# The two output products by Strassen's method, and all 22 contraction tiles of the FFNs' second products

## The chip, the cores and the metric

The kernel runs on one core of a Trainium2 chip. TensorE (PE) multiplies; VectorE (DVE), ScalarE (ACT) and GpSimd (POOL) work elementwise; SyncE (SP) and POOL issue DMAs. The metric is device time of one execution in microseconds (us), lower is better.

## The reference

One decoder layer on 512 tokens of width 1024, in fp32, batch 1: four sublayers, each followed by a normalisation of a scaled residual.

```python
def _swiglu(h, w_in, w_out):                   # w_in 1024 x 5632, w_out 2816 x 1024
    gate, up = jnp.split(h @ w_in, 2, axis=-1)
    return (jax.nn.silu(gate) * up) @ w_out

def _parallel_mixer(...):
    ...                                        # o: 4 HGRN2 heads of 128, p: 4 pooling groups of 128
    merged = jnp.concatenate([o, p], axis=-1)
    return merged @ w_out                      # 1024 x 1024

def _memory_attention(h, mem, wq, wk, wv, wo):
    q = (h @ wq)...; k = (mem @ wk)...; v = (mem @ wv)...
    p = jax.nn.softmax(s * XA_HEAD_DIM ** -0.5, axis=-1)
    o = jnp.einsum('bhsm,bmhd->bshd', p, v).reshape(b_, s_, D_MODEL)
    return o @ wo                              # 1024 x 1024

h = LN(ALPHA * h + 0.5 * _swiglu(h, ...))      # FFN1
h = LN(ALPHA * h + _parallel_mixer(h, ...))    # mixing
h = LN(ALPHA * h + _memory_attention(h, ...))  # attention into 256 memory tokens
h = LN(ALPHA * h + 0.5 * _swiglu(h, ...))      # FFN2
```

## The kernel before

**Precision.** Every fp32 operand is split in two parts: `split` (L66) lets ACT cast it to `hi` and DVE make `lo` as the difference; `mm3` and its kin then take three matmuls, hi x hi, hi x lo, lo x hi. So every tile that is to be multiplied costs one ACT and one DVE instruction of its size. `wblock` (L74) does this for a block of weights: SP loads 128 x 1024 values into a `raw` buffer (7 of them), and the two parts go to `q` buffers (7 of them, so three and a half blocks) or, with `stay`, to a large buffer (names `whi_`, `wlo_`, `ws_`).

**Order.** The program is written in one order; the framework that builds it places the instructions of each engine, follows the buffers' and data's dependencies and sets the semaphores. Each engine then works through its own list in that order. The lists are fixed before the run.

**Stages.** FFN1 (names `f1`), mixing, its output product (`mo`) with the memory keys around it (`pk`, `wk` blocks), values and queries of the attention, attention, its output product (`xo`), FFN2 (`f2`). The 512 tokens are four tiles of 128 (`h0` to `h3`), the residual is kept there, and after an output product each tile is normalised (`ln_tile`: statistics and the two linear steps on DVE, `rstd` on POOL) and transposed on PE (`trh`, L195) for the next stage.

**Output products before.** `out_gemm` (L209) takes 8 contraction tiles in 4 blocks for each half of the 1024 columns; its left side comes split already (`mg0` to `mg3`, `oT0` to `oT3`), because the steps that make it split it: the pooling groups (`pool_out`), the merge of the heads (`og`, `ot`), the attention's values (`values`). Each product is 192 matmuls of 128x512. The second half is done tile by tile, so that a tile's addition, normalisation and transposes run beside the next tile's matmuls.

**Second products of the FFNs before.** `strassen_gemm` (L317) takes Strassen's (Winograd's) form over tokens (two halves) x columns (two halves) x contraction. Seven products, in the order b11, t1, t2, b21, b22, t3, t4: the left sides are quarters `a11`, `a12`, `a21`, `a22` of the activation or sums of them made by `combine` on DVE, each split by `left` when its turn comes; the right sides are blocks of the weights (b11, b21, b22) or sums (t1 to t4) read back from DRAM. Results gather in six PSUM tiles (`u`, `v`, `w`, two each), and `add` puts them into `h`. 20 of the 22 contraction tiles go this way, in 5 blocks a product (`KB1`, `KB2`); the last two are multiplied directly by `rest` (blocks `ws`, left side `gs`), 48 matmuls between the products' ends and the additions.

**Sums.** `Sums` (L268) makes t1 to t4 in DRAM by DMAs of POOL's queue: a copy, then an accumulating DMA. Where they are issued is set by a small POOL instruction on a weight block's `hi` (`seen`): in FFN1 `step` issues four to six every other group of the first product; for FFN2 `spread` spreads its 40 over the 50 weight blocks of mixing and attention. All are issued before the second product begins.

## Time and profile before

| | |
|---|---|
| median of 3 runs | 1042.48 us (1042.39 to 1042.53) |
| the profiled execution | 1043.13 us |
| its span | 1041.4 us, 1.73 us lie around it |
| granted TensorE clock | 0.997 |
| output product of mixing, first transpose of the merge to last key | 493.3 to 557.5 us |
| attention's last value product to the first FFN2 products' end | 650.9 to 722.1 us |
| second product of FFN2 | 925.5 to 1031.0 us |

A row of the stretches gives: from and to, length, then busy us (instructions) of PE, weight loads (PEld), DVE, ACT, POOL, then the granted clock, the share of the DMA engines and GB/s. A row of waits gives: engine, what was to be written and the line, from whom it came, us in total, times, the longest. A row of the timeline gives: start, us, engine, line, operation, out<-in, shape, and in square brackets the idle time before it with its releaser. The rows of the chain give start, us, engine, what.

```profile
q1 hardware_dynamic: 38592, 128.25, 36.9%
q0 software_dynamic: 4480, 41.95, 15.9%
f2t<-in_w2out POOLq DMA_DIRECT2D x30, 512.0 KB, 6.6
```

These are the DMA queues (packets, MB, share of 16 engines' span): SP's loads above, the sums of POOL's queue below; an action of the sums for FFN2 takes 6.6 us from issue to landing.

### The profile page before, as it was taken

How to read it: one execution, taken by the hardware profiler on the slowest of the kernel's cores; microseconds unless marked ns; L12 is line 12 of the kernel's file. 1: busy time of each engine (PE TensorE's matmuls, PEld its weight loads, DVE VectorE, ACT ScalarE, POOL GpSimd, SP SyncE). 2: the span in 40 equal slices, each digit the busy share in tenths (PEclk: the TensorE clock that was granted, in tenths of full speed). 3: DMA queues.
4: the chain of work that ended last, by engine and by line, in shares of the span. 5: the costliest groups of instructions: out<-in, count | busy, mean ns of one | idle time of the engine just before them, and what ended most of it. 6: DMA issues, size and time to landing. Idle time of an engine off the chain costs nothing. (4 is left out here: it accounts for less than half of the span.)

```text
span 1041.4 us, 17704 instructions
## 1 busy us (share of the span) xinstructions
PE 1025.7 (98%) x6910; PEld 929.4 (89%) x6910; DVE 825.4 (79%) x1334; ACT 504.3 (48%) x857; POOL 95.0 (9%) x167
## 2 busy tenths in 40 slices
PE   9999999999999999999999999999999999999996
PEld 7999999998887888879888988889999999988884
DVE  6999888789898545786786356589988888889795
ACT  5656555566554331334324345226555555566530
POOL 0112211200000111102303110010000000000000
PEclk9999999999999999999999999999999999999998
DMA  9377786585665446553929871403233332436751
GB/s 364 143 236 230 222 254 212 148 247 158 216 192 182 142 155 169 148 168 82 292 72 314 273 162 41 141 22 107 97 101 122 103 101 65 139 102 202 235 189 41
DMA packets 43300, 171.59 MB, mean 165 GB/s; under 512 B 6096, under 2 KB 7376, under 8 KB 40016
## 3 DMA queue, kind: packets, MB, share of 16 engines
q1 hardware_dynamic: 38592, 128.25, 36.9%
q0 software_dynamic: 4480, 41.95, 15.9%
q8 instruction: 54, 0.88, 0.3%
q10 hardware_dynamic: 144, 0.26, 0.1%
q14 instruction: 30, 0.25, 0.1%
HBM read 168.34 MB, written 44.04 MB: 204 GB/s over the span
## 5 line engine op out<-in xcount | busy, mean ns | idle before, releaser
L177 POOL TENSOR_TENSOR rstd<-ve,mhalf 128x1 f32<-128x1 f32 x16 | 14.8, 922 | 536.1 <-DVE ve L175 536.1
L538 PE MATMUL f1u<-xt,qf1s 128*128 128x256 f32 x480 | 60.7, 283 | 0.0
L538 PE MATMUL f2u<-xt,qf2s 128*128 128x256 f32 x480 | 60.7, 283 | 0.0
L538 PEld LDWEIGHTS f1u<-xt,qf1s 128*128 128x128 f32 x480 | 59.0, 192 | 0.0
L538 PEld LDWEIGHTS f2u<-xt,qf2s 128*128 128x128 f32 x480 | 59.0, 192 | 0.0
L68 DVE TENSOR_TENSOR wlo_wv<-raw_wv,whi_wv 128x1024 fp32r<-128x1024 f32 x12 | 14.7, 1224 | 23.8 <-PE pq L57 8.5
L538 PE MATMUL f1u<-xT,qf1a 128*128 128x256 f32 x240 | 32.1, 283 | 0.0
L538 PE MATMUL f2w<-xoT,qf2a 128*128 128x256 f32 x240 | 32.1, 283 | 0.0
L538 PE MATMUL f2u<-xoT,qf2a 128*128 128x256 f32 x240 | 32.1, 283 | 0.0
L538 PE MATMUL f1w<-xT,qf1a 128*128 128x256 f32 x240 | 32.1, 283 | 0.0
L538 PE MATMUL f1v<-xt,qf1s 128*128 128x256 f32 x240 | 30.7, 283 | 0.0
L538 PE MATMUL f1u<-xt,qf1a 128*128 128x256 f32 x240 | 30.6, 283 | 0.0
L538 PE MATMUL f1v<-xT,qf1s 128*128 128x256 f32 x240 | 30.4, 283 | 0.0
L538 PE MATMUL f2v<-xt,qf2s 128*128 128x256 f32 x240 | 30.4, 283 | 0.0
L538 PE MATMUL f2v<-xoT,qf2s 128*128 128x256 f32 x240 | 30.4, 283 | 0.0
L538 PE MATMUL f2u<-xt,qf2a 128*128 128x256 f32 x240 | 30.4, 283 | 0.0
L538 PEld LDWEIGHTS f1w<-xT,qf1a 128*128 128x128 f32 x240 | 30.3, 192 | 0.1
L538 PEld LDWEIGHTS f1u<-xT,qf1a 128*128 128x128 f32 x240 | 30.2, 192 | 0.0
L538 PEld LDWEIGHTS f2w<-xoT,qf2a 128*128 128x128 f32 x240 | 30.2, 192 | 0.0
L538 PEld LDWEIGHTS f2u<-xoT,qf2a 128*128 128x128 f32 x240 | 30.2, 192 | 0.0
L538 PEld LDWEIGHTS f1v<-xt,qf1s 128*128 128x128 f32 x240 | 29.6, 192 | 0.1
L538 PEld LDWEIGHTS f1u<-xt,qf1a 128*128 128x128 f32 x240 | 29.6, 192 | 0.0
(458 smaller groups left out, 3220.3 us busy)
## 6 DMA issues: line engine op xcount, KB each, us to landing
f1t<-in_w1out POOLq DMA_DIRECT2D x30, 512.0 KB, 8.2
f2t<-in_w2out POOLq DMA_DIRECT2D x30, 512.0 KB, 6.6
raw_f1t<-f1t SPq DMA_DIRECT2D x20, 512.0 KB, 4.1
raw_f2t<-f2t SPq DMA_DIRECT2D x20, 512.0 KB, 3.9
raw_f2g<-in_w2in SPq DMA_DIRECT2D x17, 512.0 KB, 3.7
raw_f2u<-in_w2in SPq DMA_DIRECT2D x17, 512.0 KB, 3.7
raw_f1u<-in_w1in SPq DMA_DIRECT2D x15, 512.0 KB, 7.2
raw_f1b<-in_w1out SPq DMA_DIRECT2D x15, 512.0 KB, 4.8
```

What stands on the lines that cost most here:

```text
L68: nc.vector.tensor_tensor(out=lo, in0=src, in1=hi.bitcast(F32), op=ALU.subtract)
L177: nc.gpsimd.tensor_tensor(out=rstd, in0=ve, in1=mhalf[:, 0:1], op=ALU.pow)
L538: nc.tensor.matmul(o, q[:, w, wsl], x[k][r], start=opens and k == 0 and n == 0, stop=ends and k == 3 and n == 2, skip_group_check=True)
```

## The change

`out_gemm` goes. `strassen_gemm` now takes its left side as a list of `groups` and its blocks from the sums' own lists `kb1`, `kb2`, and makes all three kinds of product: `mo` and `xo` (8 contraction tiles, 2 blocks a product) and the FFNs' second ones, there with all 22 tiles: 6 blocks a product, the last one half a block (`(10, 0)` and `(10, 1)`, 512 wide). `rest`, `ws` and `gs` go. An output product now has 168 matmuls of 128x512 where it had 192; an FFN's second product has 462 for 468. The left sides stay unsplit where they are made (`mgp` from the pooling, `mgh` from the merge, `oT0`, `oT1` copied by ACT from PSUM) and are split, and combined, inside.

```diff
-    mg = {q: b8([P, 2, 2, S], F32R, f"mg{q}") for q in (2, 3)}
+    mg = [None, b8([P, 4, S], F32, "mgp")]
...
-        ov = og.rearrange("p (a b n) -> p a b n", a=2, b=2)
-        for q in range(2):
-            split(ov[:, q], mg[q][:, :, 0, cs], mg[q][:, :, 1, cs])
-
-    X2 = out_gemm(a["wmixo"], KT, mslot, ALPHA, a["ln2_g"], a["ln2_b"], LN_EPS, "mo", order=[2, 3, 0, 1])
+    X2 = strassen_gemm([(mg[1], mg[0])], sums_mo, ALPHA, a["ln2_g"], a["ln2_b"], LN_EPS, "mo")
...
-            split(po, oT[:, j, 0, :], oT[:, j, 1, :])
+            nc.scalar.copy(out=OT[hd // 2][:, 2 * (hd % 2) + j, :], in_=po)
...
-    X3 = out_gemm(a["wo"], KT, lambda k: (OT[k // 2][:, k % 2, 0, :], OT[k // 2][:, k % 2, 1, :]),
-                  ALPHA, a["ln3_g"], a["ln3_b"], LN_EPS, "xo", ys=ys,
+    X3 = strassen_gemm([OT], sums_xo, ALPHA, a["ln3_g"], a["ln3_b"], LN_EPS, "xo", ys=ys,
...
+    FFN_BLOCKS = [0, 1, 4, 5, 8, (10, 0)], [2, 3, 6, 7, 9, (10, 1)]
```

The end of `strassen_gemm`: the direct blocks stood inside `rest`, between the Strassen products and the additions.

```diff
-        def rest(t, hf, ps, opens, scale):
-
-            block(t % 2, 0, ws[hf], gs[t // 2], ps, opens, True)
-            add(t, hf, ps, scale)
+        def stats_of(t, hf):
             nc.vector.bn_stats(stats[t][:, hf, :], h[t][:, hf * 512:hf * 512 + 512])
...
         for t in range(2):
             add(2 + t, 1, u[t], False, ALU.subtract)
-            rest(2 + t, 1, mm_ps(f"{name}x{t}"), True, False)
+            stats_of(2 + t, 1)
         for t in range(2):
             for i, x in enumerate(T4):
-                block(t, i, x, L, u[t], False, False)
-            rest(2 + t, 0, u[t], False, True)
+                block(t, i, x, L, u[t], False, i == nb - 1)
+            add(2 + t, 0, u[t], True)
+            stats_of(2 + t, 0)
             done(2 + t)
```

The sums: `mo` and `xo` need 16 DMAs each, an FFN 48 (where 40 were). Their order is now t1, t3, t2 of all blocks, then t4 of all. `step` in FFN1 no longer makes t4; what is left of a product's sums is put on a list at its start and issued one behind each weight block (`one_behind` in `wblock`), t4's beside the second product itself. The list for mixing and attention holds `mo`'s sums first, then `xo`'s and FFN2's in turn.

```diff
-        for f in behind:
-            f(hi)
+        one_behind(hi)
...
+    def one_behind(hi):
+        if todo_behind:
+            seen = st.tile([P, 1], F32, tag="seen", name="seen")
+            todo_behind.pop(0)(nc.gpsimd.tensor_tensor(out=seen, in0=hi[:, 0:1].bitcast(F32), in1=mhalf[:, 0:1],
+                                                       op=ALU.mult).ins)
...
+    todo_behind += sums_mo.actions()
+    todo_behind += [x for two in zip(sums_xo.actions(), sums2.actions()) for x in two]
+    todo_behind += sums2.actions()[len(sums_xo.actions()):]
```

The order on the engines changes at two places above all. The first is the start of mixing's output product on DVE. Before, behind the key splits, stood the merge, its splits and the rest of the weight blocks, and then one addition and one statistic for each tile (`wlo_mo1_3` is the last block of the second half):

```order
L887 SCALAR_TENSOR_TENSOR og_5332<-ot_5327,gn_3873,GS_4506 128x512 [waits PE_49]
L68 TENSOR_TENSOR ws_mo1_0_5486<-raw_mo1_0_5484,ws_mo1_0_5486 128x1024 [waits DMAHW5_49]
L68 TENSOR_TENSOR mg0_5147<-og_5332,mg0_5147 128x2x128 [waits Activation_49]
L68 TENSOR_TENSOR mg1_5148<-og_5332,mg1_5148 128x2x128 [waits Activation_49]
L68 TENSOR_TENSOR wlo_mo0_3_5422<-raw_mo0_3_5419,whi_mo0_3_5421 128x1024 [waits DMAHW1_49,PE_49]
L68 TENSOR_TENSOR ws_mo1_1_5495<-raw_mo1_1_5493,ws_mo1_1_5495 128x1024 [waits DMAHW6_49]
L68 TENSOR_TENSOR ws_mo1_2_5503<-raw_mo1_2_5501,ws_mo1_2_5503 128x1024 [waits DMAHW7_49]
L68 TENSOR_TENSOR wlo_mo1_3_5509<-raw_mo1_3_5506,whi_mo1_3_5508 128x1024 [waits DMAHW0_49,PE_49,Activation_49]
L243 SCALAR_TENSOR_TENSOR h0_266<-h0_266,mops00_5351 128x512 [waits PE_49]
L246 BN_STATS stats0_5338<-h0_266 128x6 [waits DVE_49]
```

Now the left sides, combinations and additions of each product stand between the weight blocks (`moa11` and `mos1` are left sides, L292 is `combine`, `mou` the PSUM tiles of product b11):

```order
L68 TENSOR_TENSOR moa110_5415<-mgp_4350,moa110_5415 128x4x256 [waits Activation_49]
L837 SCALAR_TENSOR_TENSOR mgh_5234<-ot_5399,gn_3953,GS_4592 128x4x128 [waits PE_49]
L292 TENSOR_TENSOR mos1_5418<-mgp_4350,mgh_5234 128x1024 [waits DVE_49]
L292 TENSOR_TENSOR mgp_4350<-mgp_4350 128x4x256 [waits DVE_49]
L68 TENSOR_TENSOR mos10_5464<-mos1_5418,mos10_5464 128x4x256 [waits Activation_49]
L323 SCALAR_TENSOR_TENSOR h0_266<-h0_266,mou0_5409 128x512 [waits PE_49]
L323 SCALAR_TENSOR_TENSOR h1_267<-h1_267,mou1_5410 128x512 [waits PE_49]
L68 TENSOR_TENSOR wlo_mot10_5472<-raw_mot10_5469,whi_mot10_5471 128x1024 [waits DMAHW0_49,Activation_49]
L68 TENSOR_TENSOR wlo_mot11_5494<-raw_mot11_5491,whi_mot11_5493 128x1024 [waits DMAHW1_49,Activation_49]
```

The first block of t1 moved behind five instructions of left sides and two additions; PE takes its `lo` in the third matmul of t1. The second place is the end of t3 in the same product. On DVE the addition that frees `mou0` stands behind both normalisations and t4's blocks:

```order
L180 SCALAR_TENSOR_TENSOR h1_267<-h1_267,rstd_5687,B_5659 128x512 [waits DVE_49,Pool_49]
L180 SCALAR_TENSOR_TENSOR h1_267<-h1_267,rstd_5687,B_5659 128x512 [waits DVE_49]
L68 TENSOR_TENSOR ws_mot40_5741<-raw_mot40_5739,ws_mot40_5741 128x1024 [waits DMAHW4_49]
L68 TENSOR_TENSOR wlo_mot41_5751<-raw_mot41_5748,whi_mot41_5750 128x1024 [waits DMAHW5_49,Activation_49]
L68 TENSOR_TENSOR moT0_5757<-trh00_5761,moT0_5757 128x2x128 [waits Activation_49]
L326 TENSOR_TENSOR h2_268<-h2_268,mou0_5409 128x512
```

and on PE, from the same point, the first matmul of t4 into `mou0` waits for DVE, between the transposes of tiles 0 and 1:

```order
L192 MATMUL trh00_5761<-ident_262,h0_266 128x128 [waits DVE_49,PE_49]
L192 MATMUL trh00_5761<-ident_262,h0_266 128x128 x3
L192 MATMUL trh01_5770<-ident_262,h0_266 128x128 [waits DVE_49,PE_49]
L192 MATMUL trh01_5770<-ident_262,h0_266 128x128 x3
L56 MATMUL pk_5894<-mT0_5091,whi_wk3_5887 128x256 [waits Activation_49]
L57 MATMUL pk_5894<-mT0_5091,whi_wk3_5887 128x256
L312 MATMUL mou0_5409<-ws_mot40_5741,moa220_5736 128x512 [waits DVE_49]
L192 MATMUL trh10_5779<-ident_262,h1_267 128x128 [waits DVE_49,PE_49]
```

Nothing like this wait stood in the plain product, whose PSUM tiles `mops` each took one tile's matmuls and were then read. The end of `xo` reads alike, with tile 1's transposes ahead of t4.

More of the change, by code (lines that the diff above doesn't have):

```diff
@@ L293, in add @@
                     nc.gpsimd.dma_start(self.T[p, b], x, accum_op=ALU.add, max_dma_last_dim=8192)
-        def spread(self, hi, over, count=[0]):
-            total = 8 * NB
-            n0, n1 = (total * (count[0] + i) // over for i in range(2))
-            count[0] += 1
-            for n in range(n0, min(n1, total)):
-                seen = st.tile([P, 1], F32, tag="seen", name="seen")
-                ins = nc.gpsimd.tensor_tensor(out=seen, in0=hi[:, 0:1].bitcast(F32), in1=mhalf[:, 0:1], op=ALU.mult).ins
-                if self.copies and (n % 2 == 0 or n < 4):
-                    self.copy(ins, engine=nc.gpsimd)
-                else:
-                    self.add(ins)
@@ L308, in step, with actions @@
-        def step(self, q, n):
+        def actions(self):
+            c, a, seq = len(self.copies), len(self.adds), []
+            while a:
+                if c and a - c < 4:
+                    seq.append(self.copy)
+                    c -= 1
+                else:
+                    seq.append(self.add)
+                    a -= 1
+            return seq
+        def step(self, q):
             seen = st.tile([P, 1], F32, tag="seen", name="seen")
             ins = nc.gpsimd.tensor_tensor(out=seen, in0=q[:, 0, 0:1].bitcast(F32), in1=mhalf[:, 0:1], op=ALU.mult).ins
-            for _ in range(3 if n in (2, 4) else 2):
-                self.add(ins)
-            for _ in range(3 if n < 4 else 2):
-                self.copy(ins, engine=nc.gpsimd)
@@ L851, in layer_kernel @@
         states.append(Sn)
-    for q in range(2):
-        mg[q] = b8([P, 2, 2, S], F32R, f"mg{q}")
+    mg[0] = b8([P, 4, S], F32, "mgh")
     os_ = []
```

193 lines of the change are left out of this document (73 added, 120 removed).

## The prediction

> **What bounds the kernel now.** Four views were read: first the shares of busy time on the page, then TensorE's waits over the whole span, then the chain that ended last, and last the table of stretches around the two output products (mixing and attention).
>
> ```profile
> PE 1025.7 (98%) x6910; PEld 929.4 (89%) x6910; DVE 825.4 (79%) x1334; ACT 504.3 (48%) x857; POOL 95.0 (9%) x167
> ```
>
> ```profile
> PE idle L106 <- DVE mhalf L160: 1.1, 1, 1.1
> PE trh L195 <- issue: 0.9, 1, 0.9
> PE f2u L356 <- DVE f2a L68: 0.7, 1, 0.7
> PE f1u L356 <- DVE f1a L68: 0.7, 1, 0.7
> PE first L56 <- ACT qx L67: 0.7, 1, 0.7
> PE trh L195 <- DVE h L183: 0.7, 1, 0.7
> PE po L56 <- ACT PT L67: 0.2, 1, 0.2
> ```
>
> ```profile
> 938.53 13.60 PE f2v L356 x60
> ...
> 1014.69 16.33 PE f2u L356 x72
> 1031.03 0.02 issue
> 1031.05 0.70 DVE h L367
> ```
>
> TensorE (PE) is busy for 1025.7 of 1041.4 us and waits for data 5.0 us in all; the rest of the gap is the 10.4 us tail after its last matmul (1031.0 to the end). So a matmul taken away is worth its own time, but only as long as no other engine becomes late in that stage. A 128x512 matmul goes every 13.60 / 60 = 0.2267 us.
>
> The stretches, PE first, then weight loads, DVE, ACT, POOL, granted clock, DMA share and GB/s: the mixing output product with what remains of the memory keys (first row), and the attention output product up to the first gate and value products of FFN2 (second row).
>
> ```profile
> 493.30:557.50 64.20, 64.17 (x362) 54.99 (x361) 50.96 (x88) 22.56 (x42) 17.36 (x27) 1.00 0.62 191
> 650.90:722.10 71.20, 70.50 (x416) 61.60 (x415) 54.39 (x84) 25.81 (x39) 3.96 (x4) 1.00 0.29 97
> 938.00:952.00 14.00, 14.00 (x64) 11.58 (x63) 14.00 (x16) 9.49 (x10) 0.00 (x0) 1.00 0.64 189
> ```
>
> Both stages are PE's, but DVE already has 51.0 of 64.2 us and 54.4 of 71.2 us. The third row, a Strassen product of FFN2, shows DVE busy all the time beside PE: there one product has 60 matmuls (13.6 us) to hide its splits and combinations behind.
>
> **The change part by part.** The sum is made against the profiled execution, 1043.13 us (span 1041.4 and 1.73 around it), which lies 0.65 above the median of the runs.
>
> PE: 60 matmuls of 128x512 go: 24 in each output product (192 to 168), 6 in each FFN (468 to 462). 60 x 0.2267 = 13.6 us. If nothing else became late, the result would be 1029.5.
>
> DVE's prices are starts of one instruction to the next, back to back (us from the start of the span, then us).
>
> ```profile
> 922.79 1.22 DVE L68 TENSOR_TENSOR wlo_f2b<-raw_f2b,whi_f2b 128x1024 fp32r<-128x1024 f32 x1
> 923.92 0.42 DVE L525 TENSOR_TENSOR f2g<-f2sg,f2u 128x256 f32<-128x256 f32 x1
> 924.25 2.36 DVE L68 TENSOR_TENSOR f2a<-f2g,f2a 128x1024 fp32r<-128x1024 f32 x2
> 926.52 1.22 DVE L339 TENSOR_TENSOR f2s<-f2g,f2g 128x1024 f32<-128x1024 f32 x1
> 938.20 1.28 DVE L367 SCALAR_TENSOR_TENSOR h<-h,f2u 128x512 f32<-128x512 f32 x2
> 939.39 1.22 DVE L68 TENSOR_TENSOR wlo_f2t<-raw_f2t,whi_f2t 128x1024 fp32r<-128x1024 f32 x1
> ```
>
> 1024 elements cost 923.92 - 922.79 = 1.13 to 1.14 us, 512 elements (939.39 - 938.20) / 2 = 0.60, 256 elements 0.33. A Strassen product of the output stages has two weight blocks (2.28), one left side (1.14), often a combination (1.14) and two additions out of PSUM (1.2): 5 to 7 us of DVE beside 24 matmuls, 5.44 us of PE. The plain product had 8 weight blocks and 8 additions.
>
> Mixing's output product adds 6 weight blocks (6.84), 7 left sides (7.98), 4 combinations (4.56) and 6 additions (3.6), and drops 8 splits of 256 elements (2.64): +20.3 us, 51.0 to 71.3. PE would need 64.2 - 5.4 = 58.8. DVE becomes the longer one there. The sum alone bounds the stage from below at about 71.3 less the 2 to 3 us of DVE work that can be done before it starts: +4.7 us against 64.2.
>
> What comes late is read from the order, walked by these prices from 493.3 (t = 0), with a transpose of a tile's half at 0.5 us as an estimate from its 128-wide matmuls. The start is where DVE is free of the merge's inputs in the trace:
>
> ```profile
> 491.50 0.69 DVE L874 TENSOR_TENSOR o<-o,rs 128x512 f32<-128x512 f32 x1 [1.12 <-POOL rs L873]
> 492.11 1.22 DVE L68 TENSOR_TENSOR wlo_mo<-raw_mo,whi_mo 128x1024 fp32r<-128x1024 f32 x1
> ```
>
>  The fourth `o` is done at 492.1, 1.2 ahead of t = 0. DVE then does the low half of the second b11 block, two key splits, three multiplications of the merge and `moa11`'s low part: done at 4.1, while PE runs dry 1.2 earlier. `s1`, its split, two additions and then the first t1 block: done at 10.6, where PE came to need it at 9.2 (1.4). From t1 to b22 the two keep pace, to within half a us, and PE ends b22 at 31.9. Then DVE is behind: the last additions, statistics, `mot3` blocks, `moa22` and normalisation of tiles 0 and 1. Tile 0 is normalised at 39.1, t3 ended at 37.4, so the first transposes wait 1.75. `mou0` takes t4's product on top of t3's, so its first t4 matmul waits until DVE has read `mou0` into tile 2 (the second place of the order): after tile 1's normalisation and two t4 blocks, at 45.1, where PE is free at 40.45: 4.65 us. After t4 the transposes of tiles 2 and 3 and one key block come late by 1.1, 1.9 and 1.6. The waits sum to 1.2 + 1.4 + 1.75 + 4.65 + 1.1 + 1.9 + 1.6 = 13.6, less 5.4 of matmuls: **+8.2 us**, with +4.7 from DVE's sum alone as the lower end, and +12 as the upper, if the early products, which are within half a us, each lose another 0.7.
>
> Attention's output product: +6.84 + 7.98 + 4.56 + 3.6 less 1.2 for the two `po` splits behind the start, +21.8: 76.2 against 65.8 that PE would need, in 71.2. But 3.4 of it (two b11 blocks, `xoa11`) lies ahead, in the attention, where DVE has room:
>
> ```profile
> 610.00:648.00 38.00, 37.76 (x216) 32.65 (x216) 24.33 (x51) 19.42 (x46) 1.99 (x4) 1.00 0.35 85
> ```
>
> The same walk: t1's first block 1.7 late, tile 0's transposes 0.4, tile 1's 3.1 (they stand ahead of t4 there), `xou0` 1.2, tiles 2 and 3 3.2 together: 9.6 less 5.4, and less the 0.7 that the stage waits now (71.20 - 70.50): **+3.5 us** (0 where the work ahead of time counts in full, +8 where the sum of DVE, 76.2 + 3, paces it).
>
> FFN1 and FFN2: -6 matmuls each, -1.36. DVE gains seven weight pieces of 512 (4.2), seven left pieces and four combinations of 256 (3.6), and loses three splits of 1024 and two additions (4.6): +3.2 in all. A product's new half block also brings PE 6 matmuls, 1.36 us, against 0.60 + 0.33 + 0.33 of DVE, so nothing new waits in the products; t4's first matmul now waits for `h2 -= u` (about 0.2). In FFN1 the direct blocks stood as cover between the last tiles' additions and the transposes; without them I take +1.3 (0 to 2.6): FFN1 0, FFN2 -1.2. The t4 sums that are now made beside the second product wait for landings on POOL, where nothing else stands until the first rstd; cost 0 (up to 1).
>
> The moved sums, DMA: in mixing's product stand 14 weight blocks, 14 actions of a sum (each behind a weight block) and the two vectors, 512 KB each: 30 x 0.524 = 15.7 MB. The trace has 286 GB/s at a full queue in this stage and 355 elsewhere (the first line is the page's row of a block):
>
> ```profile
> raw_f2t<-f2t SPq DMA_DIRECT2D x20, 512.0 KB, 3.9
> ...
> 500.00:510.00 10.00, 10.00 (x45) 8.29 (x45) 7.21 (x9) 3.23 (x5) 3.88 (x6) 1.00 1.00 286
> 558.00:580.00 22.00, 22.00 (x101) 18.32 (x100) 12.22 (x13) 10.58 (x14) 5.89 (x13) 1.00 1.04 355
> ```
>
> At 355 it takes 44 us, hidden in the 51.6 us that the walk gives up to t4's end (cost 0, which I take, since the rate elsewhere shows that the queue can give it); at 286 it takes 55, 3 us above, and up to 9 where blocks come late one by one in attention's product too. POOL: `seen` and the sum's issue now stand ahead of the four `rs` of the merge and of the `rstd`s; a `seen` took 0.18 alone and 1.28 beside a DVE split:
>
> ```profile
> 492.10 1.28 POOL L302 TENSOR_TENSOR seen<-whi_mo,mhalf 128x1 f32<-128x1 f32 x1 [0.63 <-ACT whi_mo L67]
> 494.99 0.18 POOL L302 TENSOR_TENSOR seen<-whi_mo,mhalf 128x1 f32<-128x1 f32 x1 [1.07 <-ACT whi_mo L67]
> 495.38 0.82 POOL L293 DMA_DIRECT2D f2t<-f2t  x1 [0.21 <-issue]
> ```
>
> The blocks that they look at are cast some us before the `rstd`s are due, so I take 0; the upper end is one `seen` with its issue ahead of a `rstd` in each stage, 1.28 + 0.82, 2 us.
>
> Clock. Every stretch above has 1.00. Only where PE rests is it lower, 0.72 in the tail:
>
> ```profile
> 1031.00:1041.40 10.40, 0.01 (x1) 0.00 (x0) 4.39 (x8) 0.00 (x0) 0.92 (x1) 0.72 0.13 50
> ```
>
> The walk makes one gap of 4.65 and one of 3.1 us, longer than any that the trace now has. If t4's 24 matmuls ran at 0.72, they would take 7.6 instead of 5.4: +2.1 per stage. I take 0, since DVE, not PE, sets the end behind them, and keep +4.2 as the other end. The Trainium skill, in "TensorE: Matmul & The Clock Gate", Part 1 (The HAM clock gate), says that an idle window of about 3.4 us halves the clock until about 3.4 us of work have passed. By that rule a gap that covers such a window costs some 1.7 us by estimate and the sum would be +1.7 to +3.4 higher; by the trace, which has no such gap inside, nothing is shown either way beyond the tail's 0.72.
>
> Sum: 8.2 + 3.5 + 0 - 1.2 = +10.5; 1043.1 + 10.5 = 1053.6, and less the 0.65, **1053** against the median.
>
> **The rivals.** (1) Faster: DVE runs ahead, and the matmuls' time shows, -13.6 to -7, 1029 to 1036. The place is the end of each product in the two output stages: it decides once DVE gets through a product's work in less than 5.44 us, or does 12 us of it before PE needs it. For it: PE never waited for DVE for over 0.7 in this kernel, and POOL, ACT and DMA leave DVE free to start early. Against it: DVE's own starts add up to more than PE's in both stages, by 12 and 10 us, and the left sides that could be made early hang on the merge and on the last `po`. (2) Between: the stages come out near their lower ends (+4.7 and 0, with -1.4 to -2.7 of the FFNs) or somewhat better, because normalisation and splits of the last tiles pass beside the keys and the gate products: -7 to +3, 1036 to 1046. (3) Weights come late on top of the walk: at 286 GB/s raw blocks of `mot3` and `mot4` land after t = 31, where DVE is to take them, +9 and, with POOL's 2 us a stage, up to +13: 1061 to 1068. The full queue at 500 to 510 speaks for it, the 355 and the longer stage against it. (4) The clock falls in the two long gaps and t4 runs at 0.72: up to +4.2, 1056 to 1061 around a middle of 1058; against it, DVE is late behind t4 anyway. That fewer matmuls run than the change says is no rival: the order has 60 fewer.
>
> **How the numbers follow.** DVE paces both output products as walked, 1046 to 1061: 0.60, at 1053. Rival 1: 0.09. Rival 2: 0.15, of which 0.08 are faster by over 0.2%, 0.04 within it and 0.03 slower; 0.2%, 2.1 us, is about what a measurement of this kernel can tell from no change. Rival 3: 0.10. Rival 4: 0.06. Faster 0.17, same 0.04, slower 0.79. The range reaches from 1041, which leaves out rival 1 and half of rival 2, to 1066, which leaves out the far end of rival 3: 0.2 in all.
>
> **What would show it.** PE waits of `trh` and `mou`, `xou` for DVE of 1 to 5 us around the ends of t3, 11 to 14 us in mixing's stage and about 9 in attention's; the stages near 72 and 75 us; the matmuls 13.6 us less; no such waits in the FFNs; clock 1.00 in both but perhaps just behind `mou0`'s gap. It is wrong if DVE has idle time in those stages while PE waits for a DMA or POOL, if PE waits there less than 6 us together, or if FFN products begin to wait for weight halves.

## The result, and the profile after

| | before | after |
|---|---|---|
| median | 1042.43 us (1041.41 to 1042.53, 4 runs) | 1072.33 us (1070.02 to 1076.59, 4 runs) |
| ratio of after to before | | 1.0294, 95% interval 1.0257 to 1.0331 |
| profiled execution, its span | 1043.13, 1041.4 us | 1074.12, 1072.3 us |
| granted clock | 0.997 | 0.979 |

The change costs 29.9 us in the medians and 30.9 in the spans of the two profiles, on which the rest is worked. The prediction was 1053, with a range of 1041 to 1066: the sign is right, the size is not.

The table of stretches shows where the time went. The columns are: the stretch, its length, busy time of PE, weight loads, DVE, ACT and POOL, granted clock, DMA share, GB/s. The rows of after are the second product of FFN1, the output product of mixing, that of attention, the second product of FFN2 and the tail.

```profile
229.90:369.60 139.70, 134.79 (x640) 111.77 (x639) 115.06 (x154) 69.36 (x91) 19.22 (x34) 0.98 0.69 219
...
498.00:577.60 79.60, 65.41 (x339) 54.27 (x338) 69.60 (x103) 33.77 (x48) 28.91 (x44) 0.91 0.81 250
...
670.70:752.00 81.30, 71.55 (x405) 62.22 (x405) 74.75 (x105) 40.90 (x55) 21.90 (x32) 0.92 0.65 198
...
952.20:1058.00 105.80, 105.62 (x464) 86.18 (x462) 95.21 (x118) 53.91 (x64) 20.07 (x15) 1.00 0.69 220
1058.00:1072.30 14.30, 0.08 (x1) 0.00 (x0) 4.39 (x8) 0.00 (x0) 0.98 (x1) 0.64 0.09 37
```

The same stretches of before, cut at the same instructions (attention's here reaches to the first FFN2 products, 1.4 us further than the row in the prediction; mixing's row, 64.20, stands there; FFN2's second product starts with its first matmul at 923.7, not at 925.5 as the table ahead of the prediction has it):

```profile
229.90:365.00 135.10, 133.35 (x646) 111.48 (x645) 112.45 (x141) 66.16 (x80) 5.88 (x8) 1.00 0.56 179
...
650.90:723.50 72.60, 71.90 (x427) 63.00 (x426) 55.79 (x86) 26.96 (x41) 3.96 (x4) 1.00 0.29 95
...
923.70:1030.90 107.20, 106.45 (x470) 87.57 (x468) 92.47 (x105) 50.89 (x53) 2.77 (x3) 1.00 0.53 173
1030.90:1041.40 10.50, 0.11 (x1) 0.00 (x0) 4.39 (x8) 0.00 (x0) 0.92 (x1) 0.72 0.13 50
```

FFN1's second product +4.6, mixing's output product +15.4, attention's +8.7, FFN2's second product -1.4, the tail +3.8; the four stretches between differ by -0.3 to +0.1. Together 30.9. Only two of these were forecast to grow.

PE's waits over the whole span (engine, tile and line, what it waited for, us in total, times, longest):

```profile
PE trh L192 <- DVE h L180: 6.1, 3, 2.9
PE trh L192 <- ACT y L203: 4.9, 1, 4.9
PE f1u L312 <- DVE wlo_f1t L68: 3.8, 1, 3.8
PE mou L312 <- DVE h L326: 3.4, 1, 3.4
...
PE mou L312 <- ACT whi_mot L67: 1.8, 1, 1.8
```

The waits for normalised tiles (`trh`) and for `mou`'s reader are where the walk put them, and all waits together are close to it: PE is idle for 79.60 - 65.41 = 14.2 us in mixing's stretch (13.6 forecast) and 9.75 in attention's (9.6). Part of this is luck, since waits for late weight blocks (`whi_mot`), which the walk doesn't have, are among them. So the walk's waits alone don't explain the growth. Three things are beside them. First, the records hold slowed matmuls: 24 fewer of 0.2267 us should leave PE busy for 64.17 - 5.44 = 58.7 in mixing, and it is busy for 65.4. By the same reckoning 5.1 us are lost in attention's and 2.8 in FFN1's stretch, 14.6 in all. Second, FFN1 has a wait of 3.8 for a low part, `wlo_f1t`. Third, the tail is longer.

In mixing's stretch (and 3 us on either side) the DMA queues carry more than was counted. The view of DMA issues (what, queue, number, KB each, median us from issue to landing):

```profile
f2t<-in_w2out POOLq DMA_DIRECT2D x10, 512.0 KB, 7.2
xot<-in_wo POOLq DMA_DIRECT2D x9, 512.0 KB, 8.3
raw_wv<-in_wv SPq DMA_DIRECT2D x8, 512.0 KB, 6.0
raw_wk<-in_wk SPq DMA_DIRECT2D x5, 512.0 KB, 7.0
raw_mot<-mot SPq DMA_DIRECT2D x4, 512.0 KB, 14.7
raw_mob<-in_wmixo SPq DMA_DIRECT2D x3, 512.0 KB, 9.8
raw_wxq<-in_wq SPq DMA_DIRECT2D x2, 512.0 KB, 19.6
G<-in_ln_g SPq DMA_DIRECT2D x1, 512.0 KB, 15.1
B<-in_ln_b SPq DMA_DIRECT2D x1, 512.0 KB, 15.2
xot<-xot POOLq DMA_DIRECT2D x1, 512.0 KB, 8.1
f2t<-f2t POOLq DMA_DIRECT2D x1, 512.0 KB, 5.9
```

45 transfers, where the prediction counted 30 between the stage's ends. Of its 14 weight blocks only 7 are loaded here, since the loads run ahead by seven buffers. For the same reason 15 weights of the keys, values and queries that follow (`wv`, `wk`, `wxq`) are loaded here, and there are 21 actions of the sums, not 14. A block of `mot` takes 14.7 us to land. In the stretch itself ACT, which casts each block, waits 13.1 us for blocks that have not landed, and DVE waits behind it:

```profile
ACT whi_mob L67 <- DMA raw_mob<-in_wmixo: 6.3, 2, 3.4
ACT whi_mot L67 <- DMA raw_mot<-mot: 3.9, 1, 3.9
ACT ws_mot L67 <- DMA raw_mot<-mot: 2.9, 1, 2.9
DVE wlo_mot L68 <- ACT whi_mot L67: 3.1, 2, 2.1
```

Before, ACT has no wait for a DMA in this stage.

FFN1's wait is the same thing in another place. ACT's timeline (start, length, what, and in brackets the idle time before it and who ended it), then PE's:

```profile
259.80 1.05 ACT L67 CAST whi_f1t<-raw_f1t 128x1024 fp32r<-128x1024 f32 x1 [4.49 <-DMA raw_f1t<-f1t]
```

```profile
265.18 0.79 PE L312 MATMUL f1u<-wlo_f1t,f1a 128*128 128x512 f32 x1 [3.79 <-DVE wlo_f1t L68]
```

ACT waits 4.5 us for the DMA of the first block of `t2`. The low part comes 4 us later again, because the splits of the left side, which stand ahead of it on DVE, were held up with it. The DMA issues between 225 and 275 show the landings beside the sums' transfers, which the change moved into this stretch (five of the blocks, between 240 and 262, took 13.9 us), and then the landings before:

```profile
raw_f1t<-f1t SPq DMA_DIRECT2D x10, 512.0 KB, 10.8
```

```profile
raw_f1t<-f1t SPq DMA_DIRECT2D x9, 512.0 KB, 4.1
```

The tail's growth is one instruction, a drain of POOL's queue at the program's end. In the view of that line (number, then shortest, median and longest in ns, first and last start), of after and then of before:

```profile
L1008 POOLq DRAIN  x3: 40/93/11556, 1060.0 to 1072.1; - x3
```

```profile
L1062 POOLq DRAIN  x3: 40/102/7564, 1033.0 to 1041.1; - x3
```

7.56 us became 11.56, with 128 in place of 80 DMAs issued on that queue in the whole program: 4.0 us for 48, or 0.083 us each, if it goes by their number.

The theory from here: DVE paces both output products about as walked; the sums' transfers make weight blocks late in three stretches; the drain is paid for each DMA of POOL's queue. The rivals: the lowered clock behind the gaps is the cause of what the walk missed; the wait at `mou` is; or DVE's load has nothing to do with it.

### The profile page after: what moved, and what is told of

Read it like the earlier page. It is cut to its first block, busy times and chain, and to the rows that moved or that the text cites. A ratio compares the mean times of both kernels' runs of the same rounds, so it can differ in the third digit from the quotient of the medians.

```text
span 1072.3 us, 17922 instructions
## 1 busy us (share of the span) xinstructions
PE 1027.6 (96%) x6850; PEld 926.9 (86%) x6850; DVE 862.3 (80%) x1386; ACT 533.3 (50%) x897; POOL 168.5 (16%) x276
## 5 line engine op out<-in xcount | busy, mean ns | idle before, releaser
L253 POOL TENSOR_TENSOR seen<-qf2a,mhalf 128x1 f32<-128x1 f32 x10 | 4.9, 497 | 187.3 <-ACT qf2a L67 187.3
L253 POOL TENSOR_TENSOR seen<-qf1a,mhalf 128x1 f32<-128x1 f32 x10 | 5.9, 591 | 180.2 <-ACT qf1a L67 180.2
L68 DVE TENSOR_TENSOR wlo_wv<-raw_wv,whi_wv 128x1024 fp32r<-128x1024 f32 x12 | 14.7, 1223 | 22.7 <-PE pq L57 8.4
L312 PE MATMUL f1u<-whi_f1t,f1a 128*128 128x512 f32 x92 | 30.8, 410 | 0.8 <-ACT whi_f1t L67 0.8
```

Of the source, the lines that this page charges most:

```text
L68: nc.vector.tensor_tensor(out=lo, in0=src, in1=hi.bitcast(F32), op=ALU.subtract)
L253: ins = nc.gpsimd.tensor_tensor(out=seen, in0=q[:, 0, 0:1].bitcast(F32), in1=mhalf[:, 0:1], op=ALU.mult).ins
L312: nc.tensor.matmul(ps, x, y[:, csl], start=opens and k == 0 and n == 0, stop=ends and k == len(T) - 1 and n == 2, skip_group_check=True)
```

## The experiments

Each starts from the kernel before or after, as said. Ratios are to the kernel before, in runs on the same chip.

### The drain by itself

The kernel before with 48 DMAs of 2 KB added on POOL's queue:

```diff
+for i in range(48):
+    nc.gpsimd.dma_start(scr.tile([P, 4], F32, name=f"tiny{i}"), a["x"][:P, 4 * i:4 * i + 4])
```

> The kernel before, with 48 more DMAs of 2 KB each on POOL's queue in the mixing stage, to nowhere that is read. Theory: POOL's drain at the program's end grows with the number of DMAs that its queue has issued; 80 gave 7.6 us, 128 gave 11.6 us. So here the drain should be 11.6 us and the time +4.0 us against the kernel before. Rival: it grows with bytes or packets; then 7.6 us and a time within 1 us of before.

1054.02 us, ratio 1.0113 (1.0098 to 1.0128). The longest drain took 11.48 us and the tail 14.3, as in the changed kernel, though the 48 carry almost no bytes: the price is for each DMA. The total is not what was expected, because these DMAs were issued at the program's start and held POOL and the first loads there (in the first 40 us a `raw_f1g` block of 512 KB lands in 11.5 us, before in 5.9, though the 48 carry 0.1 MB together); FFN1's first product took 238.6 us instead of 229.9.

### Output products with quiet queues

The changed kernel, with no sum issued behind a block of either output product, and FFN `t4` sums not before `b21`:

```diff
-        if todo_behind:
+        if todo_behind and not hold:
...
-        todo_behind.extend(S_.actions())
+        todo_behind.extend(S_.actions(False))
...
         product(L, "t2", u, False)
+        todo_behind.extend(S_.actions(True))
...
+    hold.append(1)
     X2 = strassen_gemm([(mg[1], mg[0])], sums_mo, ALPHA, a["ln2_g"], a["ln2_b"], LN_EPS, "mo")
...
+    hold.clear()
```

The same two lines stand around attention's product, and `sums_xo` goes ahead of `sums2` in the list.

> The change, but with no sums' DMAs behind the blocks of the two output products, attention's sums ahead of FFN2's, and the FFNs' t4 sums issued only from b21 on. DMA theory: the weight blocks were late because the sums of later products share the queues; FFN1's second product goes from 139.7 to about 134 us and the waits of the two output stages (14.2 and 9.8 us) fall to under 8 together: -18 to -25 us. DVE theory: only FFN1 gains, about -6 us; the output stages keep 20 us of waits and more, the total is -6 to -10 us.

1075.37 us, ratio 1.0319 (1.0302 to 1.0336). The first two rows are the output products, the third FFN1's second product:

```profile
499.70:572.20 72.50, 61.77 (x338) 52.31 (x337) 69.23 (x103) 33.79 (x48) 13.92 (x20) 0.95 0.58 186
665.30:743.10 77.80, 70.31 (x405) 61.28 (x404) 74.67 (x105) 40.59 (x55) 3.95 (x4) 0.96 0.41 129
229.60:371.40 141.80, 134.86 (x641) 111.93 (x640) 114.67 (x155) 69.02 (x91) 29.62 (x39) 0.96 0.67 221
```

Mixing's product falls from 79.6 to 72.5 and attention's from 81.3 to 77.8, so 7.1 and 3.5 us of their growth come with the sums of other products. ACT waits for no DMA in mixing's product here. What is left, +8.3 and +5.2, is near the walk's +8.2 and +3.5. PE's waits of 10.7 and 7.5 us lie between the two forecasts (under 8 together, over 20). But nothing was won, against -6 to -25 forecast: the `t4` sums, now bunched behind `b21`, made a block of `t3` come 6.5 us late in FFN1, and FFN2's second product waited 5.7 us in all and took 114.7 us instead of 105.8. The prediction's price of 0 to 1 for sums beside a second product is refuted twice here.

The next run has the same quiet output products, and issues all of an FFN's sums in its first product, three additions and three copies a step instead of two and two, `t4` with them:

```diff
-            for _ in range(2):
-                if self.adds[0][0] != "t4":
-                    self.add(ins)
-            for _ in range(2):
-                if self.copies and self.copies[0][0] != "t4":
-                    self.copy(ins)
+            for _ in range(3):
+                self.add(ins)
+            for _ in range(3):
+                self.copy(ins)
```

> As e2 (no sums' DMAs behind the blocks of the two output products), and all 48 DMAs of each FFN's sums in its first product, t4's too, so that none runs beside a second product. Theory now: the sums' DMAs beside a stage's own blocks make these late wherever they stand (t2 in the change, t3 in e2), and what is left in the output stages is DVE. Then FFN1's second product takes 133 to 134 us, FFN2's 105 to 106, mixing's stage about 72.5, attention's about 78, the tail 14.4: +14 to +17 us against the kernel before (1056 to 1059). Rival: the FFNs' stalls come from their new half blocks and buffers; then FFN1 or FFN2 keeps a stall of 4 to 6 us and the total is +20 or more.

1069.79 us, ratio 1.026 (1.024 to 1.028), where 1056 to 1059 was expected. Mixing's product, attention's and FFN1's second product:

```profile
493.90:568.90 75.00, 64.30 (x338) 54.48 (x337) 69.40 (x103) 33.79 (x48) 12.93 (x20) 0.93 0.58 184
662.00:739.70 77.70, 70.21 (x406) 61.17 (x405) 74.69 (x105) 40.60 (x55) 3.95 (x4) 0.96 0.42 129
233.00:365.60 132.60, 132.11 (x641) 110.20 (x640) 114.63 (x155) 69.19 (x91) 7.33 (x15) 1.00 0.60 193
```

FFN1's second product is at 132.6, 2.5 below before, and its blocks of `t1` and `t2` land in 3.3 us (225 to 275):

```profile
raw_f1t<-f1t SPq DMA_DIRECT2D x10, 512.0 KB, 3.3
```

The Trainium skill, in "DMA: Bandwidth & Descriptors", section "SWDGE vs HWDGE vs iDMA", says that each DMA engine goes round between queues that POOL's transfers and SP's transfers feed apart. Loads of the same ten blocks that take 10.8 us beside the sums and 3.3 without them agree with such sharing, though no run here tells it from a limit elsewhere on the transfers' way. The time went elsewhere again: FFN1's first product grew by 3.1 us and FFN2's, which now has sums too, by 9.1 (209.3 for 200.2).

### Without the low parts of the output products' weights

This takes DVE work away. ACT casts the block and the low part is left out (`hi` stands for it), so the products are less exact and have the same matmuls:

```diff
+        if name[:2] in ("mo", "xo"):
+            hi = (b8([P, 2, n], F32R, f"ws_{name}")[:, 0, :] if stay else q4([P, n], f"whi_{name}"))
+            nc.scalar.copy(out=hi, in_=raw)
+            one_behind(hi)
+            return hi, hi
         split(raw, hi, lo)
```

First on the changed kernel:

> The change, but the two output products' weight blocks have no low part (the second matmul takes the high part again, so that part of the computation is left out and the output differs): 14 DVE instructions of 1.14 us go in each of the two stages, DMA and PE's matmuls stay. DVE theory: the waits of both stages fall from 24 us to under 8, the clock stays at 1.00 there, the total is -20 to -30 us. DMA theory: the raw blocks land as late as before, waits stay above 16 us, the total is -2 to -8 us.

1070.42 us (1060.96 to 1076.64), ratio 1.0264 (1.0203 to 1.0325): 1.9 us below the change, which is the DMA theory's side of the forecast. DVE had 56.7 us of work in mixing's product, 12.9 less, but the stage took 81.9. ACT waited 16.1 us there for the DMAs of `mot` and of a key block, and PE waited 10.5 us in one piece for a normalised tile, whose DVE work stood in line behind the low part of the key block that came 11.7 us late. So while blocks come late, less work on DVE doesn't shorten this stage; what DVE's load costs by itself this run can't tell. It shows one more thing by accident. FFN1 is the same code as in the changed kernel, and its second product took

```profile
229.20:361.80 132.60, 132.18 (x641) 110.18 (x640) 114.55 (x154) 68.89 (x91) 27.68 (x34) 1.00 0.72 230
```

7.1 us less than there. The first run of the section on the clock, with the same code again in FFN1, took 135.7. So FFN1's wait is a race between transfers, lost in one execution and won in another. The changed kernel's own four runs lie 6.6 us apart, those of the kernel before 1.1; that the race is why was not tried.

Then on the run with quiet queues and early sums:

> e5, with the low parts of the two output products' weight blocks left out as in e3 (that part of the computation is missing). With the DMAs out of the way, DVE is the only thing that can be late: DVE theory: mixing's stage 59 to 63 us and attention's 66 to 70, waits under 5 us each, clock 1.00: -6 to -10 us against the kernel before with its tail of +4 taken in (1033 to 1037). Rival (a chain of dependences, not DVE's sum, sets the stages): mixing's stage stays above 68.

1058.17 us, ratio 1.0154 (1.0139 to 1.0169). The two output products:

```profile
494.00:563.80 69.80, 62.57 (x338) 53.73 (x337) 56.37 (x89) 33.54 (x48) 11.95 (x20) 0.93 0.60 190
656.90:726.50 69.60, 67.26 (x405) 59.35 (x404) 60.56 (x92) 40.51 (x55) 3.96 (x4) 1.00 0.44 144
```

13 to 14 us of DVE work less in each stage give 5.2 us in mixing and 8.1 in attention, 11.6 in the whole. Attention came out as DVE's sum would have it (66 to 70): with its product now 3.0 us below before, DVE's load is shown to be what makes it longer. Mixing did not (59 to 63): at 69.8 us it is above the 68 that were to speak for the rival, a chain of dependences. There 7.2 us of waits are left, 5.8 of them behind t4's start, for the normalisation of the last two tiles and for a key block, and matmuls at a lowered clock (0.93) take 3.8 us more. So 5.2 of mixing's 10.8 us are shown to be DVE's load. The other 5.6 are not taken apart. The whole missed 1033 to 1037 by more than that, since the FFNs' first products keep the 3.1 and 9.6 us that the early sums cost them.

### The wait at `mou`

The run with quiet queues, with t4's product in PSUM tiles of its own (`w`), so that it need not wait until DVE has read `mou`:

```diff
-                block(t, i, x, L, u[t], False, i == nb - 1)
-            add(2 + t, 0, u[t], True)
+                block(t, i, x, L, (w if own else u)[t], own, i == nb - 1)
+            add(2 + t, 0, (w if own else u)[t], not own)
```

> e5, with t4 of the two output products in PSUM tiles of its own (w's, read by then), so that its first matmul doesn't wait until DVE has read u; two more additions of 0.6 us on DVE. If that one wait is a cause by itself: the gap of 4.9 us in mixing's stage and the 2 us of the clock behind it go, -4 to -7 us against e5 in both stages together. If DVE's sum is the cause, the wait turns up again at the next things that need DVE (transposes of tiles 2 and 3, key blocks): within 2 us of e5.

1073.46 us, ratio 1.0299 (1.0283 to 1.0315). Mixing's product took 74.8 us and attention's 77.6, both as without the edit. (The total was forecast within 2 us of that run, for this case. The 3.7 us more than there lie in the attention between them, 96.6 for 93.1.) PE now waits 4.2 us at the same place for t4's weight split and 3.0 at a key. The dependency that the walk named was the last of several to end there. Taking it away shows the next.

### The clock

The changed kernel with idle matmuls in the output products, 12 behind t3 (the expectation has 10) and 20 transposes between the first two tiles:

```diff
-        product(L, "t3", u, False)
+        w3 = product(L, "t3", u, False)
+        if len(groups) == 1:
+            for _ in range(12):
+                nc.tensor.matmul(w[0], L[3][0][:, :P], w3[0][:, 512:], start=True, stop=True)
...
                 transpose_h(t, tiles, ys)
+                if t == 0 and len(groups) == 1:
+                    for _ in range(20):
+                        nc.tensor.transpose(w[1][:, :P], h[0][:, :P], ident)
```

> The change, with idle matmuls put into the two long gaps of each output stage (10 of 128x512 behind t3 and 20 transposes behind tile 0's, to a PSUM tile that nobody reads). Clock theory: the gaps halve the clock behind them, which cost 6.7 us in mixing's stage and 5.1 in attention's; with PE busy the granted clock stays near 1.00 there and the total is -5 to -10 us. Rival: PE is not what sets the end behind the gaps (DVE is late there anyway), so the total stays within 2 us, or grows by the idle matmuls' time.

1072.02 us, ratio 1.0289 (1.0267 to 1.0311), no different from the change. Attention's clock rose from 0.92 to 0.98 and its product stayed at 81.3 us. In mixing the filling missed most of the gap (clock 0.92, 83.0 us), which left it open. So the second trial was aimed at the two long gaps of the run with quiet queues and early sums:

```diff
+        def fill(n):
+            for _ in range(n):
+                nc.tensor.matmul(w[0], L[0][0][:, :P], T4[0][0][:, :512], start=True, stop=True)
...
                 transpose_h(t, tiles, ys)
+                if t == 0 and name == "xo":
+                    fill(22)
...
+        if name == "mo":
+            fill(20)
         for t in range(2):
```

> The run with quiet queues in the output products and all FFN sums early (1069.79 us; mixing's product 75.0, attention's 77.7), with 20 idle matmuls of 128x512 put ahead of the gap of 4.9 us at `mou`'s t4 and 22 ahead of the gap of 5.55 us at the second tile's transposes in attention's product (4.5 and 5.0 us, into a PSUM tile that is read no more). In that run t4 in mixing ran for 5 us at a clock of 0.50 behind its gap, with no wait of PE for the next 15 us, and the records sum to 5.6 us of slowed matmuls in mixing's stage and 3.8 in attention's. If the clock after the gap costs time, the granted clock behind it goes to 1.00, mixing's stage falls by about 2.6 us or more (72.4 or less), attention's by 2 to 4, and the whole to about 1064 to 1066 us. If DVE sets the end of both stages whatever the clock, new waits of PE take the place of the slow matmuls: both stages within 1 us of 75.0 and 77.7, and 1069 to 1071 us.

1071.98 us, ratio 1.0278 (1.0248 to 1.0308), above both forecasts. In attention DVE's side came true. The gap shrank from 5.6 to 0.8 us, the clock rose from 0.96 to 0.98, and the product took 77.5 us against 77.7:

```profile
664.60:742.10 77.50, 74.09 (x428) 64.53 (x427) 73.54 (x104) 40.78 (x55) 3.97 (x4) 0.98 0.42 129
```

In mixing neither side came true: the product took 77.5 us, 2.5 longer than without filling. PE's waits moved; they are now

```profile
PE trh L192 <- DVE h L180: 3.7, 2, 2.0
PE mou L310 <- DVE h L324: 1.9, 1, 1.9
```

where without filling they were 0.9 and 4.9. The stretch, cut where DVE finishes the last tile's normalisation, first without and then with filling:

```profile
493.90:560.00 66.10, 56.61 (x288) 47.00 (x286) 62.78 (x94) 28.61 (x40) 8.12 (x12) 0.95 0.53 167
560.00:568.90 8.90, 7.68 (x50) 7.48 (x51) 6.62 (x10) 5.19 (x8) 4.81 (x8) 0.81 0.96 307
```

```profile
494.00:559.00 65.00, 56.62 (x283) 46.83 (x281) 61.83 (x92) 27.70 (x39) 6.45 (x10) 0.97 0.49 155
559.00:571.50 12.50, 11.00 (x75) 10.63 (x76) 7.90 (x11) 6.13 (x9) 5.47 (x10) 0.77 0.94 290
```

DVE gets there after 66.1 and 65.0 us, 1 us apart, though t4 ran at another clock. That speaks for DVE, not the clock, as what sets that end, from one execution of each. What is left behind it are keys, more of them with the filling, which took 4.5 us of PE's time (75 matmuls for 50), and at 0.77, so the stage ends later. The clock does cost something there, because PE is the bound again once DVE is through; how much of the 2.5 us between the first and the second quiet run (72.5 and 75.0) it explains was not tried.

### The 22 tiles of the FFNs alone

The last runs keep the second products with 22 tiles and the plain output products, and issue each FFN's sums, those of `t4` too, where they stood before: in its first product for FFN1 and in mixing and attention for FFN2. POOL's queue carries 96 DMAs. First, up to six a step in FFN1 (against the changed kernel, with `out_gemm` and the split left sides as before):

```diff
-    todo_behind += sums_mo.actions()
-    todo_behind += [x for two in zip(sums_xo.actions(), sums2.actions()) for x in two]
-    todo_behind += sums2.actions()[len(sums_xo.actions()):]
+    todo_behind += sums2.actions()
...
-    X2 = strassen_gemm([(mg[1], mg[0])], sums_mo, ALPHA, a["ln2_g"], a["ln2_b"], LN_EPS, "mo")
+    X2 = out_gemm(a["wmixo"], KT, mslot, ALPHA, a["ln2_g"], a["ln2_b"], LN_EPS, "mo", order=[2, 3, 0, 1])
```

> Only the FFNs' part of the change (all 22 tiles by Strassen's method), with the plain output products of before, and all sums of an FFN before its second product (FFN2's behind the blocks of mixing and attention). -1.4 us for each FFN's matmuls, +1.3 for the drain of 16 more DMAs on POOL's queue: 1041 us, -2.5 to +0.5 against the kernel before. If the new half blocks cost something by themselves: +1 to +4.

1042.54 us, ratio 1.0005 (0.9995 to 1.0014). The second products take 132.0 and 105.6 us, 3.1 and 1.6 below before. FFN1's first product gives back 2.8 and the tail 1.2. Then the same with four to five a step:

```diff
-            for _ in range(3):
+            for _ in range((0, 2, 3, 2, 3, 3, 2, 3, 3, 3)[n]):
                 self.add(ins)
-            for _ in range(3):
+            for _ in range((4, 2, 2, 3, 2, 2, 3, 2, 2, 2)[n]):
                 self.copy(ins)
```

> As in the run with the 22 tiles in the FFNs alone (plain output products, all sums in an FFN's first product), but the sums' DMAs dealt out at four to five for each step. That run gained 3.1 and 1.6 us in the second products and lost 2.8 us in FFN1's first product and 1.2 us in the drain. If the 2.8 us came from steps with six DMAs at once, FFN1's first product falls back toward 230 us and the time to about 1040 us, ratio 0.998; if it comes from their total number, nothing changes: 1042.5 us.

1039.84 us, ratio 0.9978 (0.9968 to 0.9989), the only kernel here that beats both. FFN1's first and second product, and the tail:

```profile
0.00:229.30 229.30, 227.87 (x1795) 223.43 (x1796) 199.66 (x363) 137.50 (x255) 36.65 (x63) 1.00 0.74 230
229.30:361.60 132.30, 131.84 (x639) 110.13 (x639) 114.64 (x154) 69.22 (x91) 8.25 (x17) 1.00 0.64 207
...
1025.60:1037.40 11.80, 0.14 (x1) 0.00 (x0) 4.39 (x8) 0.00 (x0) 0.92 (x1) 0.61 0.11 44
```

The same number of sums, dealt out evenly, costs FFN1's first product nothing.

### The drain in the other direction

Three runs put the plain copies on ACT's queue and leave the accumulating DMAs on POOL's. On the kernel before:

```diff
-                    self.copy(ins, engine=nc.gpsimd)
+                    self.copy(ins, engine=nc.scalar)
...
-                self.copy(ins, engine=nc.gpsimd)
+                self.copy(ins, engine=nc.scalar)
```

> The kernel before, with the 40 plain copies of its weight sums issued on ACT's queue in place of POOL's; the 40 accumulating DMAs stay on POOL's. If the drain of POOL's queue at the program's end grows with the DMAs that it carried (7.56 us with 80, 11.56 us with 128, 0.083 us for each), it falls here to about 4.2 us and the stretch behind the last product from 10.4 to about 7 us: about 1039 us, ratio 0.997. The rival is that the drain goes with the bytes or the accumulating DMAs alone: the tail stays near 10.4 us and the time near 1042 us. Against both stands ACT, whose queue now waits for POOL's little multiplication ahead of each copy: where that wait (up to 2 us) holds back an eviction, the first product of an FFN grows by up to a few us, while the tail still tells the two apart.

1046.32 us, ratio 1.0039 (1.0027 to 1.0051). The drain fell to 4.30 us and the tail to 7.8, as expected by number. But FFN1's first product took 235.3 us: all 40 copies, FFN2's too, were issued in it, FFN2's 20 long ahead of their place. On the kernel with the FFNs' 22 tiles and evenly dealt sums:

```diff
-                    nc.gpsimd.dma_start(T, x)
+                    nc.scalar.dma_start(T, x)
```

> The same with its 48 copies on ACT's queue: 48 accumulating DMAs are left on POOL's. By the count of DMAs the drain falls to about 0.9 + 48 x 0.083 = 4.9 us and the tail by 4 us against the run with the copies on POOL's queue: about 1037 to 1038.5 us, ratio 0.995 to 0.997, a version faster than both kernels. If the drain doesn't go by the count, or ACT's waits hold back evictions, it is not below 1041 us.

1042.9 us, ratio 1.0008 (0.9999 to 1.0017): tail 7.8, FFN1's first product 235.7. Last, with FFN2's 24 copies alone on ACT's queue:

```diff
-                    nc.scalar.dma_start(T, x)
+                    (nc.gpsimd if self.name == "f1" else nc.scalar).dma_start(T, x)
```

> The 22 tiles in the FFNs alone with the sums spread (1039.84 us), and the 24 copies of the second FFN's sums, which are issued in the stages between the FFNs, on ACT's queue; the first FFN's 24 stay on POOL's. The drain was 4.30, 4.95, 7.56 and 11.56 us with 40, 48, 80 and 128 DMAs on POOL's queue, so 0.083 us for each: with 72 it is 6.9 us (from 8.87), and the tail falls from 11.8 to about 9.9 us. FFN1's first product, which grew by 6 us when its own copies went to ACT's queue, stays at 229 to 230 us. In the mixing and attention, ACT's queue now waits for POOL; the runs with all copies on ACT showed no growth there (128.3, 64.2 and 93.5 us). So about 1038 us, ratio 0.996. If the copies on ACT's queue hold back its casts or transfers, it is not below 1039.8 us.

1042.08 us, ratio 1.0002 (0.9994 to 1.0011). The tail came out as forecast, 9.8 us with a drain of 6.91. FFN1's first product did not, because the 24 copies were issued in it again and filled the queues:

```profile
0.00:233.20 233.20, 229.80 (x1794) 225.29 (x1795) 199.44 (x363) 136.93 (x255) 36.09 (x63) 0.99 0.85 277
```

277 GB/s there against 230 with all copies on POOL's queue. In all three runs PE loses 2.3 to 2.7 us between 30 and 50 us, where the DMA engines are busy for 0.85 to 0.93 of the time and for 0.37 in the kernel before, and ACT never waits for POOL in that product, which was the rival. So transfers that start too early are the likely cause of all three misses, read from the traces and not tried. The tail agrees each time with the count.

## Why the prediction was wrong in size, step by step

**Output products, DVE's walk: right in kind, a little short.** With quiet queues mixing grows by 8.3 to 10.8 us (8.2 forecast) and attention by 5.1 to 5.2 (3.5). That the sizes are so close is partly luck: PE waits less there than the walk has it (10.7 us for 13.6 in mixing, 7.5 for 9.6 in attention), and matmuls at a lowered clock, which were priced at 0, fill in with 3.0 and 5.6 us in mixing and 3.8 in attention. The wait at `mou` was 4.9 there (4.65 forecast). In attention the waits that the walk spread over the last two thirds (3.1, 1.2 and 3.2) came as one, 5.6 at the second tile's transposes. Removing DVE work shortened both stages: it took away all of attention's growth, so there the mechanism is shown, and 5.2 of mixing's 10.8 us. Rival 1, in which DVE runs ahead, is out. (Its argument that PE never waited for DVE for over 0.7 overlooks the 1.1 in the first of its rows of waits; nothing hangs on it.)

**Moved sums, DMA: the step that failed first.** "Cost 0, which I take" was worked out from 30 transfers and the best rate in the trace. The stage carries 45, since weights of the next stages run ahead on the same queue, and blocks come late one by one. It cost 4.6 to 7.1 us in mixing and 3.5 in attention, the differences between the change and the two quiet runs. The prediction's own sign of being wrong came with it: DVE is idle for 10.0 us of mixing's stretch (3.3 and 5.6 with quiet queues), 3.1 of them behind casts of late blocks, and PE waits 1.8 us for such a cast. Rival 3 had this mechanism, with a chance of 0.10. Those runs also take `seen` and the issues off POOL in these stages; POOL's part in the difference (priced at 0, DVE waits once 1.4 us there for `rstd`) was not tried apart.

**t4 sums beside the second product: priced 0 to 1, took more.** FFN1's second product was forecast at 0 and came out at +4.6. With the sums elsewhere it is -2.5 to -3.1, so two steps are wrong: the cover of the direct blocks, taken as +1.3, was not needed, and the sums' transfers cost 0 to 7 as the race falls (132.6, 135.7 and 139.7 in three executions of the same code). I had asked who waits on POOL, where nothing stands, and not what shares the queue with the next raw block.

**The tail: not in the sum.** The prediction quoted the 10.4 us tail and left it as it was. It holds a drain that grows by 0.083 us for each DMA issued on POOL's queue at any time: 48 more, +3.8 to 4.0.

**The clock: priced 0; the fall is real, the price nothing in attention and open in mixing.** The granted clock fell as rival 4 said, further than to the tail's 0.72: 0.50 in the 5 us behind the gap of 4.9 us in the run with quiet queues and early sums. The Trainium skill, in "TensorE: Matmul & The Clock Gate", Part 1 (The HAM clock gate), has the clock at half after an idle window of about 3.4 us, and the trace agrees with that half. But filling the gaps gave no time back: attention's product stayed at 81.3 in the first trial and went from 77.7 to 77.5 in the second, so its slowed matmuls lie in time that PE would have waited. In mixing and in FFN1 it is not shown how much of the other 9.5 of the 14.6 us does.

**FFN2: right.** -1.4, forecast -1.2.

Against the forecast the profile's excess is 7.2 (mixing) + 5.2 (attention) + 4.6 (FFN1) - 0.2 (FFN2) + 3.8 (tail) = 20.6 us. About 12.7 to 15.2 of it came with the sums' transfers, 3.8 are the drain, and the rest, some 2 to 4, is the walk's shortfall, the clock's part included.

## What to carry to other kernels

Before a transfer is priced at nothing, count everything that shares its queues in that stretch, prefetches for later stages too, and ask which load lands next behind it and with how much slack. A product that trades matmuls for elementwise work gains only where the elementwise engine has that time inside the stage: here the FFNs' 22 tiles did (ratio 0.9978 with the sums dealt evenly), the two short products did not. And when one wait is removed, name the one that ends next, as the runs on `mou` and on the clock show.

## What the runs showed of the hardware that was not expected

The long drain of POOL's queue at the end took 4.30, 4.95, 6.91, 7.56, 8.87 and 11.56 us with 40, 48, 72, 80, 96 and 128 DMAs issued on that queue in the program, 0.0825 us for each and 1.0 beside it; 48 of 2 KB cost as much as 48 of 256 or 512 KB. And loads of 512 KB slow down beside POOL's transfers: the blocks of `mot` in mixing's product land in 3.1 and 4.5 us in the two quiet runs and took 14.7 beside the sums, those of FFN1's `t1` and `t2` 3.3 and 10.8.
